# A decoder layer on one core: the gated half's normaliser moved behind its product, and two turned tiles read from PSUM

## The chip, the core and the metric

The kernel runs on one core of a Trainium2 chip. The core has a matrix engine (PE, TensorE), three engines for element-wise work (DVE or VectorE, ACT or ScalarE, POOL or GpSimd), a queue for transfers (SP) and 16 DMA engines. PE writes into PSUM, which has eight banks; the other data lies in SBUF. The engines run side by side, each takes its own list of instructions in order, and they wait for one another by semaphores.

The metric is device time in microseconds (us), as the median of several runs. All comparisons are on the same core.

## The reference, cut to what matters

Sequence 512, width 1024, one batch, one layer, float32 throughout. The mixing width is halved: 8 heads of block-sparse attention (512 columns) and a chunked gated unit (gMLP, 512 columns).

```
h = x @ w_in ; q, k, v, u, z = split(h)                 # u, z: 512 columns each
attn = moba_attention(rope(q), rope(k), v)
u, z = gelu(u), gelu(z)
sg = u * (tril(w_s) @ layer_norm(z) + b_s)              # spatial gating, chunks of 128
merged = concat(rms_norm(attn, attn_g), rms_norm(sg, gmlp_g))
x1 = layer_norm(ALPHA * x + merged @ w_out, ln1)        # ALPHA = 2 ** 0.25
ffn = (silu(x1 @ w_gate) * (x1 @ w_up)) @ w_down        # hidden 2816
out = layer_norm(ALPHA * x1 + ffn, ln2)
rms_norm(a, g) = a * rsqrt(mean(a ** 2) + 1e-6) * g     # over the 512 columns, per token
```

The normaliser of a token is one number. It can be multiplied into the token's row of `sg` before the product with `w_out`, or into the row of the product behind it; the gain `g` belongs to a column of `sg` and has to be in before.

## The kernel before

**Products.** Every float32 operand X is split into two parts of a faster matmul type: hi = X rounded (on ACT, L241) and lo = X - hi (on DVE or POOL, L242). A product is three matmuls, hi by hi, lo by hi and hi by lo (`mm3`, L252). Weights arrive by DMA as a tile `wr` of 128x1024 and are split into `wh` and `wl` by class `W` (L260). The table `WHI` names the weights whose hi part is made on DVE instead (L239), the table `WPOOL` those whose lo part is made on POOL. Names in these tables: `o0` to `o7` are the eight weight tiles of `w_out`, `q0` to `q3` those of the four pairs of heads, `z` those of the z projection.

**Order.** No instruction's place is written by hand. Functions only describe operations with their engine, a cost and the tiles they read and write; `Order.plan` (L110) then lists them. It walks a planned time forward, and whenever an engine comes free it takes, among the operations that are ready, the one with the smallest rank (`RANK`, with the place in the program as tie-break). Its costs, the handover between engines (`CROSS`), the ranks and the order of the parts (`SEQ`) are numbers at the top of the file. What comes out is one fixed list for each engine.

**Parts.** v first, then, by `SEQ`: `q0` to `q3` project and rotate (`qk_proj`, rope on DVE, SP and POOL), `a0` to `a3` are attention for two heads each, `z` and `u` project and apply GELU, `s` is the spatial unit. Projections fill PE while attention goes through DVE and ACT.

**The spatial unit (L554).** For each of four pairs of groups PE computes six small products into a bank `pj`, and DVE adds the bias and multiplies by u in place (L569, twice a pair, tile `ug`, tokens on partitions).

**The normaliser (`gmlp_norm`, L580).** For each of the four token tiles t: ACT squares the row and sums it (L587), DVE adds eps (L283), POOL takes the power -1/2 (L284), DVE scales the row by it and by the gain (L589), PE turns the 128x512 tile (four transposes, L594), and the turned tile is split into `znh` on ACT and `znl` on DVE (L241, L242). Only then can the product with the lower half of `w_out` begin for that t (`out_half(4, ...)`, L657). Its result is added to ALPHA times the residual `xk` (L651).

**Output product, attention's half (L784)** and the first LayerNorm: `pa_done` (L755) scales the product and adds it (L759), takes statistics (L696), POOL takes the power (L284), ACT normalises (L709), DVE multiplies the gain (L711), and the bias is added on POOL or DVE (L720) by the letter of `LN1` for the tile: "P" is POOL, "A" is DVE. Each half is turned by PE into a bank `tp` or `pv` (L769), copied by ACT into SBUF (`XR`, L773), and for some split from the bank.

**The feed-forward part** is a Strassen-like scheme: tiles 0 and 1 (`b11`, `b21`) are used alone in the first products of a pair (`p1`, `p2`), combinations of all four tiles (`n1`, `n2`, `t3`, `t4`, made in `combine`, L737) in the later ones. `p1` fills a bank and ACT copies it (L875) before `p2` adds to the same bank. Early weights get their lo part by a POOL-issued accumulating DMA (L250).

## Time and profile before

| | us |
|---|---|
| median of 3 runs (lowest to highest) | 559.56 (559.43 to 560.99) |
| the profiled execution | 557.63 |
| its span in the trace | 555.9 |
| PE busy in the span | 542.1 |
| DVE, ACT, POOL busy | 411.2, 285.8, 155.8 |

The span is the time from the first to the last instruction of the trace; the profiled execution's own time is 1.7 us longer. PE is the engine to look at: whatever its list waits for is time, and whatever the other engines do while it does not wait is not. PE works in a pipeline, so its rows overlap: the distance between two starts is what a matmul costs when nothing is waited for. The same holds, by less, for DVE and ACT.

### The profile page before, as it was taken

What the parts mean: (1) busy time and instruction counts of PE and PEld (TensorE: products, weight loads), DVE (VectorE), ACT (ScalarE), POOL (GpSimd) and SP (SyncE); (2) the same over time, 40 slices, a digit from 0 to 9 for tenths busy, and PEclk for the clock granted to TensorE, in tenths of its full rate; (3) what the DMA queues carried; (4) which work ended last, traced back from release to release, by engine and by line L of the source; (5) the groups of instructions that cost most, each with busy time, mean ns of one, the idle gap of its engine ahead of it and who ended that gap; (6) DMA issues with size and microseconds to landing.
All of it is one profiled execution on the core that took longest, in us unless ns stands there. A gap on an engine that the chain in (4) does not pass through costs nothing.

```text
span 555.9 us, 8789 instructions
## 1 busy us (share of the span) xinstructions
PE 542.1 (98%) x3360; PEld 484.7 (87%) x3360; DVE 411.2 (74%) x703; ACT 285.8 (51%) x488; POOL 155.8 (28%) x120
## 2 busy tenths in 40 slices
PE   9999999999899999999999999999999999999994
PEld 5888888888588899999999999999999888888883
DVE  5557779879986899989988878878877532324475
ACT  6323796788874698544454544454455332232211
POOL 0016248804203541144443324224233100000010
PEclk9999999999999999999999999999999999999998
DMA  7744423145723996344433233233223423223222
GB/s 249 257 156 150 137 70 101 52 155 174 259 58 115 268 220 193 121 146 152 151 114 116 77 114 115 80 130 98 73 77 122 143 78 113 85 105 100 90 75 75
DMA packets 22953, 71.80 MB, mean 129 GB/s; under 512 B 3072, under 2 KB 3584, under 8 KB 22912
## 3 DMA queue, kind: packets, MB, share of 16 engines
q1 hardware_dynamic: 22048, 68.11, 37.4%
q0 software_dynamic: 864, 3.15, 3.1%
q8 instruction: 26, 0.43, 0.3%
q14 instruction: 15, 0.12, 0.1%
HBM read 64.95 MB, written 2.10 MB: 121 GB/s over the span
## 4 chain that ended last, share of the span: by engine, by line
PE 95%; ACT 2%; DVE 1%; DMA 1%; issue 0%; DVEq 0%; ACTq 0%
PE pj L853 22%; PE sc L853 16%; PE pj L254 12%; PE pj L256 12%; PE pj L255 12%; PE sc L255 3%; PE sc L256 3%; PE sc L254 3%; PE pv L491 2%; PE tp L474 2%; PE sc L436 1%; PE pv L256 1%; PE tp L255 1%; PE pv L255 1%; PE tp L256 1%; PE pv L254 1%
## 5 line engine op out<-in xcount | busy, mean ns | idle before, releaser
L242 DVE TENSOR_TENSOR wl<-wr,wh 128x1024 fp32r<-128x1024 f32 (+1 forms) x56 | 69.9, 1249 | 62.1 <-ACT wh L241 61.7
L241 ACT ACTIVATE wh<-wr 128x1024 fp32r<-128x1024 f32 (+1 forms) x58 | 57.8, 999 | 84.2 <-PE sc L256 54.0
L853 PE MATMUL pj<-qk,wh 128*128 128x256 f32 x352 | 64.3, 283 | 0.0
L853 PE MATMUL sc<-xh,wh 128*128 128x256 f32 x352 | 64.3, 283 | 0.0
L284 POOL TENSOR_TENSOR sm<-sm,only 128x1 f32<-128x1 f32 (+2 forms) x17 | 16.9, 993 | 141.9 <-DVE sm L283 139.2
L853 PEld LDWEIGHTS pj<-qk,wh 128*128 128x128 f32 x352 | 54.9, 192 | 0.0
L853 PEld LDWEIGHTS sc<-xh,wh 128*128 128x128 f32 x352 | 54.9, 192 | 0.0
L853 PE MATMUL pj<-V,wh 128*128 128x256 f32 x288 | 52.9, 284 | 0.7 <-ACT cs L875 0.7
L853 PE MATMUL pj<-qk,wl 128*128 128x256 f32 x176 | 49.8, 283 | 0.0
L853 PE MATMUL sc<-xh,wl 128*128 128x256 f32 x176 | 49.8, 283 | 0.0
L254 PE MATMUL pj<-wh,xh 128*128 128x512 f32 x114 | 46.7, 410 | 0.0
L853 PEld LDWEIGHTS pj<-V,wh 128*128 128x128 f32 x288 | 44.9, 192 | 0.9 <-ACT cs L875 0.9
L255 PE MATMUL pj<-wl,xh 128*128 128x512 f32 x114 | 44.6, 391 | 0.0
L853 PE MATMUL pj<-V,wl 128*128 128x256 f32 x144 | 40.8, 284 | 0.0
L256 PE MATMUL pj<-wh,xl 128*128 128x512 f32 x96 | 37.8, 394 | 0.0
L242 POOL TENSOR_TENSOR wl<-wr,wh 128x1024 fp32r<-128x1024 f32 x7 | 17.2, 2459 | 73.4 <-ACT wh L241 50.6
L241 ACT ACTIVATE wh<-tp 128x512 fp32r<-128x512 f32 x33 | 19.7, 596 | 29.9 <-PE sc L853 20.4
L853 PEld LDWEIGHTS pj<-qk,wl 128*128 128x128 f32 x176 | 33.8, 192 | 0.0
L853 PEld LDWEIGHTS sc<-xh,wl 128*128 128x128 f32 x176 | 33.8, 192 | 0.0
L853 PE MATMUL sc<-ug,wh 128*128 128x256 f32 x176 | 32.3, 283 | 1.0 <-ACT wh L241 1.0
L242 DVE TENSOR_TENSOR wl<-tp,wh 128x512 fp32r<-128x512 f32 x33 | 22.6, 684 | 8.3 <-ACT wh L241 8.0
L853 PEld LDWEIGHTS sc<-ug,wh 128*128 128x128 f32 x176 | 27.5, 192 | 1.3 <-ACT wh L241 1.2
(349 smaller groups left out, 1511.0 us busy)
## 6 DMA issues: line engine op xcount, KB each, us to landing
wr<-w_dn SPq DMA_DIRECT2D x22, 512.0 KB, 3.3
wr<-w_gu SPq DMA_DIRECT2D x20, 512.0 KB, 4.1
zg<-w_gu SPq DMA_DIRECT2D x18, 512.0 KB, 3.3
kl<-w_gu SPq DMA_DIRECT2D x14, 512.0 KB, 3.3
wr<-w_vqk SPq DMA_DIRECT2D x8, 512.0 KB, 3.3
wr<-w_zu SPq DMA_DIRECT2D x8, 512.0 KB, 3.2
wr<-w_out SPq DMA_DIRECT2D x8, 512.0 KB, 4.3
wr<-w_vqk SPq DMA_DIRECT2D x8, 256.0 KB, 4.4
```

The costliest lines, as they stand in the source:

```text
L241: act(n, lambda: A.activation(hi(), src(), AF.Copy), rs, ws_hi, **k)
L242: either("P" if far else "D", n, lambda E: E.tensor_tensor(out=lo(), in0=src(), in1=hi().bitcast(F32), op=ALU.subtract), [*rs, *ws_hi], ws_lo,
L254: PE.matmul(o(), lhsT=lh(), rhs=rh(), start=start, stop=False)
L255: PE.matmul(o(), lhsT=lh(), rhs=rl(), start=False, stop=False)
L256: PE.matmul(o(), lhsT=ll(), rhs=rh(), start=False, stop=stop)
L284: od.op("POOL", 0.3 + 0.165 * n, lambda: PL.tensor_tensor(out=o.t, in0=v.t, in1=mhalf.t[:, :n], op=ALU.pow), [v, mhalf], [o], lock=True)
L436: PE.matmul(sc.t[:, :n], lhsT=qs.t[:, e, ts], rhs=ks.t[:, 2 * e + 1, :n], start=False, stop=True)
L474: PE.transpose(tp.t[:, j * P:j * P + P], p.t[:, j * P:j * P + P], ident.t)
L491: PE.matmul(pv.t[:, j * P:], lhsT=vs.t[:, j, h, :], rhs=pt.t[:, j * S:j * S + w], start=j == 0 and i == 0, stop=j == NT - 1 and i == 1)
L853: PE.matmul(o, lhsT=lh(w), rhs=buf.t[:, s + rh, x], start=first and side == k == i == 0, stop=k == 3 and i == 2, skip_group_check=True)
```

## The change

1. **Normaliser.** `gmlp_norm` goes. Right after each spatial pair j, `gmlp_turn(j)` turns the pair's 128 columns for all four token tiles (PE, L588), and splits them with the gain as a column scale: hi on ACT (L591), lo on DVE (L592). `gmlp_rms(t)` computes the sum of squares (ACT, L598) and the factor `rg` = 1 / (ALPHA rms) (DVE L601, POOL L603) beside that. The factor is applied behind the product: `xk` becomes product times `rg` plus the residual without ALPHA (L653). To fit, attention's factor `ra` also carries 1/ALPHA and the first LayerNorm's eps is divided by ALPHA squared. The gain moves from a row (`rowp`, 768 to 512 KB) to four columns (`colp`).
2. **PSUM.** For token tiles 2 and 3 `XR` is the bank itself: four copies (L773) go, and `combine` reads the banks `tp` and `pv`. It uses two SBUF tiles for n1 and n2 and computes t3 and t4 in place; the number of DVE operations in it stays.
3. **Tables.** `CROSS`, `SEQ`, `RANK`, `LNT`; `LN1` from "PAPA" to "PPPP" (bias of tiles 1 and 3 on POOL); `WHI` without `o1`, `o2` (hi part on ACT); `WPOOL` with `o5` and `q2` (lo part on POOL).

```diff
-SAME, CROSS, DMA_LAT, MM, MMD, MM256 = 0.15, 0.19, 1.9, 0.643, 0.681, 0.36
+SAME, CROSS, DMA_LAT, MM, MMD, MM256 = 0.15, 0.15, 1.9, 0.643, 0.681, 0.36
-SEQ = ('q1', 'a1', 'q0', 'z', 'q2', 'a0', 'u', 'q3', 's', 'a2', 'a3')
+SEQ = ('q1', 'q0', 'a1', 'z', 'q2', 'a0', 'u', 'a2', 'q3', 's', 'a3')
-LN1, LN2, LNT = "PAPA", "ADAD", 0.05
-WHI = ('o0', 'o1', 'o2', 'o3', 'q1')
-WPOOL = ('o1', 'o2', 'o4', 'z')
+LN1, LN2, LNT = "PPPP", "ADAD", 0.3
+WHI = ('o0', 'o3', 'q1')
+WPOOL = ('o1', 'o2', 'o4', 'o5', 'q2', 'z')
...
         for g2 in range(G // 2):
             pair(g2)
-    def gmlp_norm():
...
-            act(512, lambda: A.activation(sq.t, z(), AF.Square, accum_out=ss.t), [ug], [sq, ss], acc=True)
-            rsqrt_col(rs, lambda: ss.t, [ss], 1, 1.0 / 512, RMS_EPS)
-            dve(512, lambda: V.scalar_tensor_tensor(out=z(), in0=z(), scalar=rs.t, in1=rowp.t[:, 2, :], op0=ALU.mult,
-                                                    op1=ALU.mult), [rs, rowp, ug], [(ug, ("t", t))], lock=True)
...
+            gmlp_turn(g2)
+    sgh, sgl = [work([P, NT, S], tag, 1, F32R) for tag in ("znh", "znl")]
+    rg = small(NT)
+    def gmlp_turn(j):
+        tp, keys, g = pj(), [(ug, ("g", 2 * j)), (ug, ("g", 2 * j + 1))], lambda: colp.t[:, 12 + j:13 + j]
+        def turn():
+            for t in range(NT):
+                PE.transpose(tp.t[:, t * P:t * P + P], ug.t[:, t, j * P:j * P + P], ident.t)
+        pe(0.45, turn, [*keys, ident], [tp])
+        act(512, lambda: A.activation(sgh.t[:, j, :], tp.t, AF.Copy, scale=g()), [tp, colp], [(sgh, j)], aps=1)
+        dve(560, lambda: V.scalar_tensor_tensor(out=sgl.t[:, j, :], in0=tp.t, scalar=g(), in1=sgh.t[:, j, :].bitcast(F32),
+                                                op0=ALU.mult, op1=ALU.subtract), [tp, colp, (sgh, j)], [(sgl, j)])
+    def gmlp_rms(t):
+        sq, ss = tmp(), small(1)
+        act(512, lambda: A.activation(sq.t, ug.t[:, t, :], AF.Square, accum_out=ss.t), [ug], [sq, ss], acc=True,
+            base=RANK["sq2"])
...
-                dve(560, lambda: V.scalar_tensor_tensor(out=xk.t[:, t, hs], in0=xk.t[:, t, hs], scalar=ALPHA,
-                                                        in1=b[hf].t, op0=ALU.mult, op1=ALU.add),
+                dve(560, lambda: V.scalar_tensor_tensor(out=xk.t[:, t, hs], in0=b[hf].t, scalar=rg.t[:, t:t + 1],
+                                                        in1=xk.t[:, t, hs], op0=ALU.mult, op1=ALU.add),
...
-            xr = XR[i, t] = prob() if t < 2 else tmp()
-            act(512, lambda: A.activation(xr.t, tp.t, AF.Copy), [tp], [xr])
+            xr = XR[i, t] = prob() if t < 2 else tp
+            if t < 2:
+                act(512, lambda: A.activation(xr.t, tp.t, AF.Copy), [tp], [xr])
```

The lists of the engines move with it. PE's list holds the same 3358 matmuls before and after. It differs only in the stretch that ran from 49 to 245 us; before and behind that it is the same work in the same order (but for a few neighbours near the end).

PE, where the last of the spatial work meets the output product. Before: `tp_1533` is attention's turn, `pj_1541` and `pj_1585` are the turned tiles of t = 0 and 1, `pj_1566` is the output product of t = 0.

```order
L474 MATMUL tp_1533<-only_1_206,pr_1424 128x128 x3
L594 MATMUL pj_1541<-only_1_206,ug_1205 128x128 x4
L254 MATMUL pj_1566<-wh_1330,znh_1551 128x512
L255 MATMUL pj_1566<-wl_1358,znh_1551 128x512
L256 MATMUL pj_1566<-wh_1330,znl_1556 128x512
L254 MATMUL pj_1566<-wh_1408,znh_1551 128x512
L255 MATMUL pj_1566<-wl_1451,znh_1551 128x512
L256 MATMUL pj_1566<-wh_1408,znl_1556 128x512
L474 MATMUL tp_1582<-only_1_206,pr_1445 128x128
L594 MATMUL pj_1585<-only_1_206,ug_1205 128x128 x4
```

The same place now: `pj_1547` is the last spatial pair (its first three matmuls are its first group, the next three its second), `pj_1568` its turned columns, `pj_1581` the output product of t = 0.

```order
L474 MATMUL tp_1531<-only_1_208,pr_1391 128x128 x3
L254 MATMUL pj_1547<-znh_1000,wh_1271 128x256
L255 MATMUL pj_1547<-znl_1021,wh_1271 128x256
L256 MATMUL pj_1547<-znh_1000,wl_1376 128x256
L588 MATMUL pj_1568<-only_1_208,ug_1200 128x128 x4
L474 MATMUL tp_1576<-only_1_208,pr_1425 128x128
L254 MATMUL pj_1581<-wh_1389,znh_1561 128x512
L255 MATMUL pj_1581<-wl_1410,znh_1561 128x512
L256 MATMUL pj_1581<-wh_1389,znl_1574 128x512
```

The last spatial pair now stands directly ahead of the turn that needs it, and the turn directly ahead of the output product.

DVE at the same place. Before, from the first L589 on (`kl`, `rt`, `xh`, `atr`, `pr` belong to attention, `zg_1598` and `wl_1593` to the weights of `w_out`):

```order
L369 TENSOR_TENSOR rt_1512<-pj_1412,cs_199 128x512
L589 SCALAR_TENSOR_TENSOR ug_1205<-ug_1205,sm_1508,only_6_221 128x512
L462 RECIPROCAL sm_1528<-sm_1503 128x1
L370 TENSOR_TENSOR rt_1539<-pj_1412,cs_191 128x512
L668 SCALAR_TENSOR_TENSOR xh_1526<-atr_827,only_5_218,xh_1526 128x512 x2
L242 TENSOR_TENSOR znl_1556<-pj_1541,znh_1551 128x4x128
L283 TENSOR_SCALAR sm_1562<-sm_1547 128x1
L497 TENSOR_TENSOR atr_827<-atr_827,pv_1516 64x512
L242 TENSOR_TENSOR ptl_1573<-tp_1533,pth_1559 128x3x128
L589 SCALAR_TENSOR_TENSOR ug_1205<-ug_1205,sm_1570,only_6_221 128x512
L242 TENSOR_TENSOR wl_1593<-wr_1410,wh_1578 128x1024
```

Now (the L670 is the former L668):

```order
L450 ISA pr_1510,sm_1511<-sc_1440,only_2_213 128x256
L462 RECIPROCAL sm_1525<-sm_1507 128x1
L670 SCALAR_TENSOR_TENSOR xh_1495<-atr_726,only_5_220,xh_1495 128x512 x2
L370 TENSOR_TENSOR rt_1538<-pj_1327,cs_193 128x512
L462 RECIPROCAL sm_1544<-sm_1535 128x1
L409 TENSOR_TENSOR kl_1478<-rt_1364,kl_1478 64x512
L569 SCALAR_TENSOR_TENSOR ug_1200<-pj_1547,only_5_220,ug_1200 128x4x64
L497 TENSOR_TENSOR atr_726<-atr_726,pv_1515 64x512
L569 SCALAR_TENSOR_TENSOR ug_1200<-pj_1547,only_5_220,ug_1200 128x4x64
L242 TENSOR_TENSOR ptl_1566<-tp_1531,pth_1542 128x3x128
L592 SCALAR_TENSOR_TENSOR znl_1574<-pj_1429,only_5_220,znh_1561 128x512
L592 SCALAR_TENSOR_TENSOR znl_1574<-pj_1451,only_5_220,znh_1561 128x512
```

L589 and the wide `wl` are out of the way (that `wl` is on POOL now), and the last pair's two L569 stand behind attention's rows.

PE at the start of the feed-forward part, where `p2` of pair 2 (bank `pj_2347` before) begins. Before, `p2` of pair 1 (`pj_2257`) stood ahead of it:

```order
L853 MATMUL pj_2257<-V_2153,ptl_2026 128x256 x2
L853 MATMUL pj_2257<-V_2153,znl_2012 128x256
L853 MATMUL pj_2347<-V_2153,wh_2211 128x256 x2
L853 MATMUL pj_2347<-V_2153,wl_2224 128x256
```

Now the last rows of `p1` of that pair (`pj_2348`, weights `wh_2152`) stand three matmuls of pair 3 (`pj_2439`) ahead of its `p2` (weights `wh_2227`):

```order
L859 MATMUL pj_2348<-V_2141,wh_2152 128x256 x2
L859 MATMUL pj_2348<-V_2141,wl_2169 128x256
L859 MATMUL pj_2439<-V_2141,wh_2266 128x256 x2
L859 MATMUL pj_2439<-V_2141,wl_2276 128x256
L859 MATMUL pj_2348<-V_2141,wh_2227 128x256 x2
L859 MATMUL pj_2348<-V_2141,wl_2242 128x256
```

Between the end of `p1` and the start of `p2` on one bank there were 16 rows of another pair before, and there are two now.

POOL at the same time. Before:

```order
L284 TENSOR_TENSOR sm_2112<-sm_2109,only_7_73 128x1
L720 TENSOR_TENSOR xl_1510<-xl_1510,kl_1822 128x512 x2
L250 DMA wl_2173<-w_gu 128x1024
L284 TENSOR_TENSOR sm_2233<-sm_2229,only_7_73 128x1
L250 DMA wl_2224<-w_gu 128x1024
L284 TENSOR_TENSOR sm_2273<-sm_2267,only_7_73 128x1
L720 TENSOR_TENSOR xl_1510<-xl_1510,kl_1822 128x512 x2
L250 DMA wl_2284<-w_gu 128x1024
```

Now:

```order
L284 TENSOR_TENSOR sm_2105<-sm_2102,only_7_73 128x1
L722 TENSOR_TENSOR xl_1497<-xl_1497,kl_1828 128x512 x4
L250 DMA wl_2169<-w_gu 128x1024
L284 TENSOR_TENSOR sm_2200<-sm_2187,only_7_73 128x1
L722 TENSOR_TENSOR xl_1497<-xl_1497,kl_1828 128x512 x2
L250 DMA wl_2242<-w_gu 128x1024
L284 TENSOR_TENSOR sm_2295<-sm_2286,only_7_73 128x1
L250 DMA wl_2276<-w_gu 128x1024
L722 TENSOR_TENSOR xl_1497<-xl_1497,kl_1828 128x512 x2
```

The bias of all four tiles is on POOL, and that of the last tile stands behind a DMA issue.

## Rows read from the trace of the kernel before

**Rows 1.** Busy time by stretch: width, then busy us and (instructions) of each engine.

```profile
core 0: us, PE busy (x) PEld busy (x) DVE busy (x) ACT busy (x) POOL busy (x), PEclk, DMA share, GB/s
40.00:130.00 90.00, 90.00 (x457) 76.07 (x456) 71.39 (x175) 64.19 (x123) 48.32 (x32) 1.00 0.36 110
...
140.00:150.00 10.00, 7.26 (x34) 5.06 (x34) 9.53 (x17) 9.84 (x20) 2.40 (x3) 1.00 0.82 268
...
220.00:230.00 10.00, 9.31 (x76) 9.03 (x76) 9.94 (x17) 5.33 (x10) 2.40 (x1) 1.00 0.20 57
...
250.00:540.00 290.00, 290.00 (x1979) 270.64 (x1978) 200.77 (x256) 120.56 (x186) 67.75 (x51) 1.00 0.32 105
```

**Rows 2.** Waits of PE: total us, times, longest.

```profile
PE pj L255 <- DVE sm L283: 1.3, 1, 1.3
...
PE sc L853 <- ACT wh L241: 1.0, 1, 1.0
PE pj L254 <- ACT znh L241: 1.0, 1, 1.0
PE pj L853 <- ACT cs L875: 0.7, 1, 0.7
PE pj L594 <- DVE ug L589: 0.3, 1, 0.3
```

**Rows 3.** Timeline, 141 to 146 us: start, duration, engine, line, tile.

```profile
141.91 0.50 PE L256 MATMUL pj<-wh,znl 128*128 128x512 f32 x1
...
144.11 1.81 DVE L242 TENSOR_TENSOR wl<-wr,wh 128x1024 fp32r<-128x1024 f32 x1 [0.47 <-ACT wh L241]
...
145.97 0.50 PE L255 MATMUL pj<-wl,znh 128*128 128x512 f32 x1 [1.34 <-DVE sm L283]
```

**Rows 4.** Timeline of DVE, 130 to 143 us.

```profile
130.53 0.48 DVE L569 SCALAR_TENSOR_TENSOR ug<-pj,only,ug 128x256 f32<-128x256 f32 x1
130.93 0.55 DVE L242 TENSOR_TENSOR ptl<-tp,pth 128x384 fp32r<-128x384 f32 x1
...
139.85 1.40 DVE L668 SCALAR_TENSOR_TENSOR xh<-atr,only,xh 128x512 fp32r<-128x512 f32 x2
141.18 0.68 DVE L242 TENSOR_TENSOR znl<-pj,znh 128x512 fp32r<-128x512 f32 x1
```

**Rows 5.** Timeline of PE, 129 to 132 us.

```profile
129.64 0.28 PE L254 MATMUL pj<-znh,wh 128*128 128x256 f32 x1
...
130.00 0.28 PE L254 MATMUL pj<-znh,wh 128*128 128x256 f32 x1
```

**Rows 6.** Timeline of PE around 224 and 240 us.

```profile
223.78 0.28 PE L853 MATMUL pj<-V,wl 128*128 128x256 f32 x1
224.75 0.50 PE L853 MATMUL pj<-V,wh 128*128 128x256 f32 x2 [0.69 <-ACT cs L875]
...
239.27 0.28 PE L853 MATMUL sc<-xh,wl 128*128 128x256 f32 x1
240.56 0.48 PE L853 MATMUL sc<-ug,wh 128*128 128x256 f32 x2 [1.01 <-ACT wh L241]
```

**Rows 7.** Timeline of POOL, 205 to 210 us.

```profile
206.80 2.70 POOL L720 TENSOR_TENSOR xl<-xl,kl 128x512 f32<-128x512 f32 x2
209.45 0.87 POOL L250 DMA_DIRECT2D wl<-w_gu  x1
```

**Rows 8.** Timeline of DVE and POOL where they meet, 50 to 54 and 204 to 208 us.

```profile
50.31 2.39 POOL L242 TENSOR_TENSOR wl<-wr,wh 128x1024 fp32r<-128x1024 f32 x1 [0.93 <-ACT wh L241]
...
50.78 2.46 DVE L403 TENSOR_TENSOR qk<-rt,qk 64x512 fp32r<-64x512 f32 x1 [0.60 <-ACT qk L402]
...
53.34 0.69 DVE L403 TENSOR_TENSOR qk<-rt,qk 64x512 fp32r<-64x512 f32 x1
...
204.44 0.15 DVE L700 SCALAR_TENSOR_TENSOR sm<-sm,sm 128x1 f32<-128x1 f32 x1
...
207.02 1.26 DVE L700 SCALAR_TENSOR_TENSOR sm<-sm,sm 128x1 f32<-128x1 f32 x1
```

More of the change, by code (lines that the diff above doesn't have):

```diff
@@ L576, in spatial @@
             pair(g2)
-    SG = {}
-    def gmlp_norm():
-        sgh, sgl = work([P, NT, S], "znh", 1, F32R), work([P, NT, S], "znl", 1, F32R)
-        def one(t):
-            ts = slice(t * P, t * P + P)
-            z = lambda: ug.t[:, t, :]
-            sq, ss, rs, tp = tmp(), small(1), small(1), pj()
-            act(512, lambda: A.activation(sq.t, z(), AF.Square, accum_out=ss.t), [ug], [sq, ss], acc=True)
-            rsqrt_col(rs, lambda: ss.t, [ss], 1, 1.0 / 512, RMS_EPS)
-            dve(512, lambda: V.scalar_tensor_tensor(out=z(), in0=z(), scalar=rs.t, in1=rowp.t[:, 2, :], op0=ALU.mult,
-                                                    op1=ALU.mult), [rs, rowp, ug], [(ug, ("t", t))], lock=True)
-            def turn():
-                for j in range(4):
-                    PE.transpose(tp.t[:, j * P:j * P + P], ug.t[:, t, j * P:j * P + P], ident.t)
-            pe(0.45, turn, [(ug, ("t", t)), ident], [tp])
-            split(512, lambda: tp.t.rearrange("p (j c) -> p j c", c=P), lambda: sgh.t[:, :, ts],
-                  lambda: sgl.t[:, :, ts], [tp], [(sgh, t)], [(sgl, t)], lock=False)
-        for t in range(NT):
-            one(t)
-        SG[0] = (sgh, sgl)
+            gmlp_turn(g2)
@@ new lines, in gmlp_rms @@
+    def gmlp_rms(t):
+        sq, ss = tmp(), small(1)
+        act(512, lambda: A.activation(sq.t, ug.t[:, t, :], AF.Square, accum_out=ss.t), [ug], [sq, ss], acc=True,
+            base=RANK["sq2"])
+        v = small(1)
+        dve(1, lambda: V.tensor_scalar(v.t, ss.t, ALPHA ** 2 / 512, ALPHA ** 2 * RMS_EPS, op0=ALU.mult, op1=ALU.add),
+            [ss], [v], base=RANK["sq2"])
+        od.op("POOL", 0.465, lambda: PL.tensor_tensor(out=rg.t[:, t:t + 1], in0=v.t, in1=mhalf.t[:, :1], op=ALU.pow),
+              [v, mhalf], [(rg, t)], lock=True, base=RANK["sq2"])
@@ L612, in s_part @@
         spatial()
-        gmlp_norm()
+        for t in range(NT):
+            gmlp_rms(t)
     parts = {"z": z_part, "u": lambda: gelu(ug, tok_proj(4)), "s": s_part}
@@ L686, in build, with layer_norm @@
     HV = [slice(0, 512), slice(512, 1024)]
-    def layer_norm(t, add, done, how):
+    def layer_norm(t, add, done, how, eps=LN_EPS):
         keys = [(xk, (t, 0)), (xk, (t, 1))]
@@ L780, in pa_done @@
         od.base = RANK["ln"] + LNT * t
-        layer_norm(t, add, done, LN1[t])
+        layer_norm(t, add, done, LN1[t], LN_EPS / ALPHA ** 2)
         od.base = RANK["fill"]
```

48 lines of the change are left out of this document (25 added, 23 removed).

## The prediction, made before the changed kernel was run

> **What bounds the kernel now.** I read the busy time by stretch first, to see where PE does not work. It is busy for 90.00 of 90 us from 40 to 130 us and for 290.00 of 290 from 250 to 540 [rows 1]. The change moves nothing behind 245 us, so nothing can be won or lost there but by carrying a delay along. In the stretch that the change touches, PE is short only from 140 to 150 us, 7.26 of 10, and by a little from 220 on, as 9.31 of 10 [rows 1]. Second come the waits of PE [rows 2]: 1.3, 1.0 and 0.3 us belong to the 140s, 0.7 and 1.0 to the start of the feed-forward part. Idle time alone is too small a count, since PE's rows also stretch: at 141.91 a matmul stands 0.5 us behind the one before it, because its `znl` was just being made. By start distances beyond the usual 0.227 us per matmul, my working from the whole stretch gives 4.2 us lost from 140 to 150, against the 2.74 that are idle [rows 1]. From 220 to 245 it gives 2.3: 0.85 between 223.78 and 224.75 (0.97 less the usual 0.12), 1.17 between 239.27 and 240.56, and 0.3 in small pieces [rows 6].
>
> So at most 4.2 + 2.3 = 6.5 us can come back, out of 557.63. The profile says in the same row what else holds the 140s: DVE is busy for 9.53 and ACT for 9.84 of 10 us there [rows 1]. That the normaliser's chain stands in PE's way is true, but the engines behind it are full.
>
> **The normaliser.** Off the path go four L589 and the three operations ahead of each. PE still needs the turned tile and its split. What takes the chain's place is the last spatial pair: bias and gate on DVE (L569), turn, hi on ACT, lo on DVE, then the product. I walked DVE's new list from the first L569 to the eighth, on which the last turn waits. It holds eight L569 at 0.40 (start to start, [rows 4]), two L670 at 0.665 (the pair of 1.33, 139.85 to 141.18, [rows 4]), two L409, L369, L370, L497 and one whole-width `ptl` at about 0.6 like the other whole-width rows, and some fifteen shorter rows of attention that come to 2.8 in all: 3.2 + 1.3 + 3.7 + 2.8 = 11.0 us. PE has between the end of the first group of products and that turn: seven groups at 0.36 [rows 5] or 2.5, three projection products at 0.68 or 2.0, 1.3 for three turns of `ug`, 1.1 for attention's turns, 0.7 for scores and 1.2 for a `mix`: 8.8 us. DVE is late by 11.0 - 8.8 = 2.2, with handovers 2.35. Before it, PE waits some 0.8 for attention's own `pth` and `tp`, behind it some 0.4, among that 0.15 for the `wl` of `o5`, which POOL now makes in 2.39 [rows 8] and DVE made in 1.81 [rows 3]. Sum 3.6 against 4.2: **-0.6 us**. The wait is turned over from ACT, POOL and DVE in a row to DVE alone. Bounds: DVE's rows of attention could slip behind the last L569 no further, since the list is fixed, but the walk's sum is off by a tenth either way, and ACT's four L591 in a row could come 1 us late. I take -2.5 to +1.0.
>
> The rest of the normaliser is hidden. L598, L601 and L603 come behind, POOL's power of one column takes about what it did, and `rg` is needed only when the first product of t = 0 is done, eight products later. L653 has as many operands as L651. The smaller DMA for `rowp` lands long before z is normalised. If that cover were gone, the price were one chain, ACT to POOL, once.
>
> **PSUM.** Four ACT copies of some 0.5 go. ACT at 204 to 214 is full, so they are worth having there, but PE did not wait for `n1` and the others: combine ran some 2.4 us ahead of its products. The banks `tp` and `pv` are kept longer, until `n1` and `n2` are made; the turns of tile 3 stand further back now and that covers it. I take 0, between -0.5 and +0.5. A whole-width DVE row that reads a bank takes 0.68 [rows 4] and one that reads SBUF alone 0.69 [rows 8], so the source adds nothing that I can see.
>
> **The start of the feed-forward part.** Two things get worse. The bias of tiles 1 and 3 moves from DVE, where it took some 0.65 each, to POOL at 2.70 for two [rows 7], and for tile 3 behind a DMA issue of 0.87 [rows 7]: I count 0.4 us for a turn that waits. And `p2` of pair 2 comes three matmuls behind its `p1` instead of sixteen rows. The place at 224 us shows what a `p2` directly behind its `p1` costs, 0.85 [rows 6]. Of that the three matmuls cover 0.36, which leaves 0.5 if ACT is free. The other two waits stay: pair 3 has the same 0.85, and the one at 240.56 comes to about 1.05 against 1.17. Sum: 0.4 + 0.5 - 0.1 = **+0.8 us**, between -0.5 (the turns aren't late, and ACT's copy is out in time) and +2.0 (both and ACT behind by another copy).
>
> **Order of attention.** From 49 to 130 us PE waits for nothing today [rows 1]. In the new list the scores of the first attention come some 4.7 us earlier against their chain of POOL's add, ACT and DVE's split and a transfer. I get 2 us of slack there and 0.8 at one weight later. I take 0, between -0 and +1.5, as there is nothing to win.
>
> **Sum.** 557.63 - 0.6 + 0 + 0.8 + 0 = 557.8. The profiled execution lies 1.93 under the median of 559.56, so the forecast is 559.8.
>
> **Rivals.** First, the chain really was the wait and DVE's queue is not one: the eighth L569 is out in time, PE loses some 1 us where it lost 4.2, and the start of the feed-forward part comes to nothing: 559.56 - 3.2 = 556.4. If the later waits go too, 554.5. For it: the whole ACT, DVE, POOL, DVE, PE, ACT loop is gone, DVE has 9.7 us less to do in all, and the turns for the first three pairs are done while attention still runs. Against it: DVE's share of 9.53 [rows 1], and that the new list puts L670, L370 and L409 ahead of the last pair.
>
> Second, slower: POOL's added work holds DVE. At 50.78 a DVE row of two SBUF tiles took 2.46 us beside POOL's L242, and 0.69 for the next one without it; at 207.02 a row of one column took 1.26 beside POOL's L720, and 0.15 without [rows 7, 8]. The change gives POOL three more L242 and four more bias additions in the first LayerNorm. Each can hold such a DVE row, by 1.77 and by 1.11. It decides where PE waits for DVE, which is at the last spatial pair (one low half) and in the LayerNorm (two more pairs of additions): 1.77 + 2 x 1.11 = 4.0, of which I take three quarters as uncovered, 3.0, as 559.8 + 3.0 = 562.8. Against it: L569 and L592 read a bank and only one SBUF tile, so that only L670, L409 and the like are hit.
>
> [...]
>
> Third, the same side with another mechanism: the scores of the first attention come before their transfer, 1 to 1.5 us at most, 561. It lies within the range.
>
> **How the numbers follow.** A run of this kernel can be told from no change by about 0.3%, or 1.7 us. My forecast (wait turned over, +-1.7 around 559.8, cut at the same bound) gets 0.43. The first rival gets 0.35, since the walk's term of 2.35 is a difference of two sums of 11 and 9. The second gets 0.17 and the third 0.05 beyond the bound. So faster 0.35, within 0.3% 0.43, slower 0.22. The range runs from 555.3, with the better part of the first rival in it, to 562.4, which leaves out some 0.1 on each side.
>
> **What will show it.** PE's busy share in the stretch of the last L588: 7 of 10 if I am right, over 9 if the first rival is. The wait of PE L588 on DVE L569 should be near 2 us, with L670, L370 and L409 in DVE's timeline directly ahead of it without a gap. At the start of the feed-forward part the wait for the copy `cs` (now L881) should stand twice, 0.5 and 0.7. If DVE rows of 1.2 to 2.5 us stand beside POOL's L242 or L722 ahead of a wait of PE, it is the second rival. The forecast is wrong if L588 does not wait, or if waits arise from 49 to 130 us.

## The result, and the profile after

The changed kernel takes 563.69 us (median of four runs, 563.28 to 565.04). The kernel before, run beside it, takes 559.98 (559.43 to 560.99). The ratio is 1.0071, with an interval of 1.0053 to 1.0088: 3.7 us slower, where no change was forecast. The range ended at 562.4, so the time lies outside it, and the side it came out on had been given a chance of 0.22. The versions further down were each run beside the kernel before, at other times than the changed kernel, so that their ratios to it compare better than their times. One run in all, of the version with two mends, took 672.07 at a mean clock of 0.75, a slow state, and is left out of its median.

The profiled execution of after took 563.28, its span is 561.6, against 557.63 and 555.9 before: the two traces differ by 5.7 us, the medians by 3.7. The trace of before is of an execution 2.3 us under its median, that of after of one 0.4 under. So the traces are good for finding places and sizes, and 2 us of their difference is not the change's.

The page's list of busy times, engine by engine:

```profile
PE 545.4 (97%) x3360; PEld 486.5 (87%) x3360; DVE 404.4 (72%) x690; ACT 285.8 (51%) x486; POOL 169.0 (30%) x127
```

DVE has 6.8 us less to do than before (411.2), ACT the same, POOL 13.2 more (155.8). PE is busy for 3.3 us longer with the same products. That is the first sign: an engine whose work is the same is busier only if single rows take longer or overlap less, as behind the wait at 144.00, where an L254 takes 0.38 that takes 0.28 elsewhere [rows 5].

The waits of PE in after, as total us, times, longest (before: [rows 2]):

```profile
PE pj L859 <- ACT cs L881: 2.0, 3, 0.9
PE pj L588 <- DVE ug L569: 1.6, 1, 1.6
...
PE pj L254 <- DVE rt L370: 0.7, 1, 0.7
PE tp L474 <- DVE ptl L242: 0.7, 2, 0.5
PE pv L491 <- ACT pth L241: 0.5, 1, 0.5
```

Counted as the prediction counts (start distances beyond the usual ones, my working over the whole trace), PE loses 18.3 us in after and 12.6 in before. The difference of 5.7 is the whole difference of the spans, and it lies in these places (where a stretch is cut moves up to 0.3 between neighbours):

| stretch | before | after | difference | forecast |
|---|---|---|---|---|
| first 10 us | 1.2 | 1.6 | +0.4 | 0 |
| 80 to 100 us, attention | 0.5 | 1.1 | +0.6 | 0 (0 to +1.5) |
| 130 to 160 us, spatial unit and output product | 5.5 | 7.65 | +2.15 | -0.6 (-2.5 to +1.0) |
| 200 to 250 us, start of the feed-forward part | 2.75 | 5.4 | +2.65 | +0.8 (-0.5 to +2.0) |
| all the rest | 2.65 | 2.55 | -0.1 | 0 |

Behind 250 us nothing is lost, as before: PE is busy for 280.00 of 280 us from 260 to 540.

**The spatial unit.** The timeline of PE, 144 to 151 us (start, duration, engine, line, tile, and in brackets the idle time ahead and what ended it):

```profile
144.00 0.38 PE L254 MATMUL pj<-znh,wh 128*128 128x256 f32 x1 [0.74 <-DVE rt L370]
...
146.53 0.66 PE L588 MATMUL pj<-only,ug 128*128 128x128 f32 x4 [1.56 <-DVE ug L569]
...
147.65 0.79 PE L254 MATMUL pj<-wh,znh 128*128 128x512 f32 x1 [0.16 <-DVE znl L592]
148.24 0.63 PE L255 MATMUL pj<-wl,znh 128*128 128x512 f32 x1
148.67 0.63 PE L256 MATMUL pj<-wh,znl 128*128 128x512 f32 x1
...
150.69 0.39 PE L255 MATMUL pj<-wl,znh 128*128 128x512 f32 x1
150.92 0.40 PE L256 MATMUL pj<-wh,znl 128*128 128x512 f32 x1
```

And that of DVE behind which PE waits:

```profile
137.50 0.88 DVE L569 SCALAR_TENSOR_TENSOR ug<-pj,only,ug 128x256 f32<-128x256 f32 x2 [0.88 <-PE pj L256]
...
141.95 1.40 DVE L670 SCALAR_TENSOR_TENSOR xh<-atr,only,xh 128x512 fp32r<-128x512 f32 x2
143.26 0.68 DVE L370 TENSOR_TENSOR rt<-pj,cs 128x512 f32<-128x512 f32 x1
...
144.04 0.69 DVE L409 TENSOR_TENSOR kl<-rt,kl 64x512 fp32r<-64x512 f32 x1
145.00 0.48 DVE L569 SCALAR_TENSOR_TENSOR ug<-pj,only,ug 128x256 f32<-128x256 f32 x1 [0.28 <-PE pj L256]
...
146.00 0.47 DVE L569 SCALAR_TENSOR_TENSOR ug<-pj,only,ug 128x256 f32<-128x256 f32 x1
...
146.86 2.71 DVE L592 SCALAR_TENSOR_TENSOR znl<-pj,only,znh 128x512 fp32r<-128x512 f32 x4
```

L670, L370 and L409 stand in a row from 141.95 to 144.73 ahead of the last pair's L569, as the walk had it. But they do not hold that L569. Behind them DVE stands idle for 0.28 and waits for PE's last product of the pair. What they hold is PE, which does not start the pair until 144.00, when L370 has ended. By that it needed the bank that L370 was still reading: each turned tile keeps a `pj` bank until its L592, and the four L592 come only behind the last L569. So 0.91 is lost ahead of the pair, to DVE's queue. The 1.72 ahead of the turn are mostly the pair's own road: PE's list puts the turn behind the pair with nothing between, and both L569 (0.41 and 0.47) have to come first. Of DVE's queue only L497 stands between them, with 0.59.

Then the windows. They give width, then busy us and (instructions) of PE, PEld, DVE, ACT and POOL, then the granted clock, the DMA share and GB/s:

```profile
140.00:144.00 4.00, 2.49 (x14) 1.73 (x14) 3.99 (x12) 3.77 (x9) 0.00 (x0) 1.00 0.60 180
144.00:147.00 3.00, 1.44 (x10) 1.18 (x10) 2.69 (x7) 2.98 (x6) 0.90 (x1) 1.00 0.81 243
147.00:148.00 1.00, 0.84 (x4) 0.49 (x3) 1.00 (x2) 1.00 (x3) 1.00 (x1) 0.56 0.93 340
148.00:150.00 2.00, 2.00 (x6) 1.52 (x6) 2.00 (x6) 2.00 (x6) 1.82 (x3) 0.50 0.92 311
150.00:151.00 1.00, 1.00 (x5) 0.82 (x4) 1.00 (x2) 0.97 (x3) 0.47 (x1) 0.73 0.67 229
140.00:150.00 10.00, 6.77 (x30) 4.92 (x31) 9.69 (x24) 9.74 (x21) 3.71 (x3) 0.86 0.76 241
```

From about 147.1 to 150.5 the granted clock is 0.50. In PE's rows it is the distance of 0.43 between products that otherwise stand 0.23 apart (148.24 to 148.67, against 150.69 to 150.92). The six distances from 147.65 to 150.37 take 2.72 us where six of 0.227 take 1.36: about 1.4 us. (Some expectations below still count eight products and 1.6.) In the trace of before the same ten microseconds have a clock of 1.00 [rows 1]. Of the +2.15 in this stretch, then, about 1.4 are the clock and 0.8 are waits.

**The start of the feed-forward part.** PE's three waits for the copy between two products on one bank:

```profile
218.97 0.50 PE L859 MATMUL pj<-V,ptl 128*128 128x256 f32 x2 [0.61 <-ACT cs L881]
...
224.50 0.51 PE L859 MATMUL pj<-V,wh 128*128 128x256 f32 x2 [0.47 <-ACT cs L881]
...
231.03 0.50 PE L859 MATMUL pj<-V,wh 128*128 128x256 f32 x2 [0.87 <-ACT cs L881]
```

By starts they cost 0.77, 0.63 and 1.03. Before there was one such wait, 0.85 [rows 6]. The first is new altogether. ACT, ahead of it:

```profile
214.19 1.51 ACT L711 ACTIVATE xl<-xl,sm,sm 128x512 f32<-128x512 f32 x2
215.71 1.28 ACT L886 ACT_TABLE_LOAD   x1
217.00 0.38 ACT L886 ACTIVATE sqa<-pj 128x256 f32<-128x256 f32 x1
217.28 0.62 ACT L241 ACTIVATE xh<-pr 128x512 fp32r<-128x512 f32 x1
217.81 0.62 ACT L241 ACTIVATE ug<-pr 128x512 fp32r<-128x512 f32 x1
218.33 0.59 ACT L881 ACTIVATE cs<-pj 128x512 f32<-128x512 f32 x1
```

The last product of that `p1` ended at 216.20. Its copy starts 2.1 us later. Behind the normalising of two half tiles (L711, done at 215.70) ACT loads a table, applies SiLU to a half tile (both L886) and makes two splits, in a row without a gap. The twelve rows of PE between `p1` and `p2`, 18 matmuls in 2.2 us, did not cover that.

### The profile page after: what moved, and what is told of

Read it like the earlier page. It is cut to its first block, busy times and chain, and to the rows that moved or that the text cites. A ratio compares the mean times of both kernels' runs of the same rounds, so it can differ in the third digit from the quotient of the medians.

```text
span 561.6 us, 8778 instructions
## 1 busy us (share of the span) xinstructions
PE 545.4 (97%) x3360; PEld 486.5 (87%) x3360; DVE 404.4 (72%) x690; ACT 285.8 (51%) x486; POOL 169.0 (30%) x127
## 4 chain that ended last, share of the span: by engine, by line
PE 89%; DVE 5%; ACT 2%; DMA 2%; issue 1%; POOL 1%; DVEq 0%; ACTq 0%
PE pj L859 20%; PE sc L859 17%; PE pj L254 11%; PE pj L256 11%; PE pj L255 11%; PE sc L255 2%; PE sc L256 2%; PE sc L254 2%; DMA wr<-w_gu 2%; PE tp L474 1%; PE pv L491 1%; PE sc L435 1%; PE sc L436 1%; PE pv L256 1%; PE tp L255 1%; PE pv L255 1%
## 5 line engine op out<-in xcount | busy, mean ns | idle before, releaser
L242 DVE TENSOR_TENSOR wl<-wr,wh 128x1024 fp32r<-128x1024 f32 (+1 forms) x53 | 65.4, 1234 | 19.4 <-ACT wh L241 19.0
L241 ACT ACTIVATE wh<-wr 128x1024 fp32r<-128x1024 f32 (+1 forms) x60 | 59.8, 997 | 38.1 <-PE sc L255 7.2
L284 POOL TENSOR_TENSOR sm<-sm,only 128x1 f32<-128x1 f32 (+2 forms) x13 | 14.9, 1148 | 127.2 <-DVE sm L283 127.1
L254 PE MATMUL pj<-wh,xh 128*128 128x512 f32 x114 | 47.1, 413 | 0.0
L242 POOL TENSOR_TENSOR wl<-wr,wh 128x1024 fp32r<-128x1024 f32 x10 | 23.9, 2398 | 45.9 <-ACT wh L241 30.1
L241 ACT ACTIVATE wh<-tp 128x512 fp32r<-128x512 f32 x33 | 19.7, 596 | 30.3 <-PE sc L859 20.4
L242 DVE TENSOR_TENSOR wl<-tp,wh 128x512 fp32r<-128x512 f32 x33 | 22.6, 684 | 8.3 <-ACT wh L241 7.8
```

The lines of the kernel that those rows point to most:

```text
L241: act(n, lambda: A.activation(hi(), src(), AF.Copy), rs, ws_hi, **k)
L242: either("P" if far else "D", n, lambda E: E.tensor_tensor(out=lo(), in0=src(), in1=hi().bitcast(F32), op=ALU.subtract), [*rs, *ws_hi], ws_lo,
L254: PE.matmul(o(), lhsT=lh(), rhs=rh(), start=start, stop=False)
L284: od.op("POOL", 0.3 + 0.165 * n, lambda: PL.tensor_tensor(out=o.t, in0=v.t, in1=mhalf.t[:, :n], op=ALU.pow), [v, mhalf], [o], lock=True)
```

## The experiments

The theory after the two traces was: (a) the idle time at 140 to 146.5 us is DVE's queue, as the walk had it, and the lower clock behind it adds to the cost; (b) the start of the feed-forward part pays for copies that ACT makes late. The rivals: the tables alone are bad; the PSUM part is the cost; POOL's added work holds DVE; and whatever wait is removed, the next queue takes it over.

### New code with the old tables

The code of after, with `CROSS`, `SEQ`, `RANK` (and 10.0 for the new entry `sq2`), `LNT`, `LN1`, `WHI`, `WPOOL` of before.

> The changed code (normaliser behind the product, tiles 2 and 3 read from PSUM) under the tables of before (CROSS, SEQ, RANK, LN1, LNT, WHI, WPOOL; the new rank sq2 set to 10.0). Theory A, the loss sits in where the tables put things: this is level with or faster than before, 556 to 560 us, the waits at 219, 231 and 246 us of the changed kernel shrink to about 2 us in all, and PE's granted clock does not fall. Theory B, the loss sits in the code (the last spatial pair waits for DVE's queue whatever the tables): 562 to 564 us, a wait of PE on L569 of 1.5 us or more, and a clock below 1.00 behind it.

570.56 us, ratio 1.0186 (1.0166 to 1.0207). The clock stays at 1.00 from 130 to 160 us, though the turn waits just as long (1.6); PE is busier around it, 8.09 us from 140 to 150 against 6.77 in after. The loss lies elsewhere, at the first LayerNorm. Waits of PE:

```profile
PE tp L774 <- ACT xl L711: 4.1, 1, 4.1
...
PE tp L774 <- POOL xl L722: 1.5, 1, 1.5
```

Neither theory had these two waits of L774. Behind the longer one the clock falls here too: its mean from 207 to 214 us is 0.51. What follows is that the new code does not come out faster with the old numbers either, and that one wait's length does not settle whether the clock falls.

### Old code with the new tables

> The code of before under the new tables. Theory A (tables): 562 to 565 us, with the waits for the copy cs at the start of the feed-forward part as in the changed kernel, 2 us. Theory B (code): 559 to 561 us. If both halves lose, it is worse than before by about half of 3.7 us, near 562.

575.76 us, ratio 1.028 (1.025 to 1.0309). Waits of PE:

```profile
PE tp L474 <- DVE ptl L242: 7.4, 5, 2.7
```

The window of 140 to 160 us:

```profile
140.00:160.00 20.00, 12.99 (x48) 10.34 (x48) 16.43 (x33) 14.78 (x32) 4.59 (x6) 0.66 0.66 221
```

Attention's turns wait five times, and the clock is 0.66 on average. It falls twice more, to means of 0.57 from 214 to 222 us and 0.51 from 259 to 266. The tables cost 15.8 us on the old code, the code 10.6 on the old tables, both together 3.7. They belong to each other, and neither half alone tells what the other is worth.

### The PSUM part alone

The kernel before, with the two turned tiles read from their banks and the new `combine`.

> Before with tiles 2 and 3 read from PSUM and nothing else changed. My forecast put this at 0 with bounds of -0.5 and +0.5 us: 559.5 to 560.5 us. A rival says that banks tp and pv held longer make the turns of tile 3 wait: +0.5 to +1.5 us, with a wait of PE on DVE at about 212 us.

561.29 us, ratio 1.0018 (1.0005 to 1.0031): about 1.0 us slower, where 0 was forecast. `p2` now waits twice for its copy, and a turn waits 0.84 at 202.51 for a split on DVE. That turn is of the second tile. The banks that are held longer come in only with the four turns from 211.31 to 216.55, and none of these waits. Ahead of the split ACT had stood idle before a weight's hi part (timeline of ACT):

```profile
199.70 1.06 ACT L248 ACTIVATE wh<-wr 128x1024 fp32r<-128x1024 f32 x1 [1.11 <-PE pj L255]
```

Waits of PE:

```profile
PE pj L857 <- ACT cs L879: 1.4, 2, 0.7
...
PE pv L772 <- DVE V L242: 0.8, 1, 0.8
```

The lists of the 140s read as those of before, and yet the clock fell there in this execution, as the window shows:

```profile
140.00:150.00 10.00, 7.45 (x26) 5.23 (x27) 9.45 (x17) 9.68 (x20) 2.55 (x3) 0.83 0.81 266
```

So a part of the 1.0 us may be the clock, and not the banks.

### All but the PSUM part

Its complement: the changed kernel with the four copies and the `combine` of before.

> The changed kernel without its PSUM part: tiles 2 and 3 copied to SBUF by ACT (L773 of before) and combine as before; new normaliser and new tables. By e4, where the PSUM part alone cost 1.0 us (interval 0.3 to 1.7), it should win about 1 us: 562.7. If the tables only fit the lists with the PSUM part, it loses: 564 to 567.

563.16 us, ratio 1.0058 (1.0036 to 1.008), 0.5 under after. `L588` waits 1.6 here too, `cs` twice, 0.9 in all. The interval overlaps that of after, so 0.5 cannot be told from nothing. By the medians of these two versions the PSUM part carries 0.5 to 1.0 of the 3.7 (0 to 1.7 with the intervals), and the normaliser with its tables the rest.

### Filling the idle time, in the turn's own bank

Six more matmuls, whose result nobody reads, ahead of the last turn.

```diff
         def turn():
+            if j == 3:
+                for _ in range(6):
+                    PE.matmul(tp.t, lhsT=vs.t[:, 0, 0, :], rhs=vs.t[:, 0, 0:4, :], start=True, stop=True)
             for t in range(NT):
```

> The changed kernel with six more matmuls of 512 columns (1.4 us at full clock) into the bank of the last turn of ug, ahead of that turn, in the time in which PE waits for L569; the turn overwrites them, and every other instruction stands as it did. Theory: the granted clock of 0.50 from 147.3 to 150.4 us follows from that idle time, so with PE busy the clock stays at 1.00 and the eight matmuls that were 0.2 us late each are on time: 1.6 us less, about 562.0 us. Rival: the clock falls anyway, or the added matmuls delay the turn by as much: 563.5 us or more.

566.75 us, ratio 1.0117 (1.0098 to 1.0136). A miss, and an instructive one: the bank is freed only with L569, so that the fill waited where the turn had waited, and then ran itself at the lower clock (timeline of PE).

```profile
145.78 2.93 PE L589 MATMUL pj<-V 128*128 128x512 f32 x6 [1.56 <-DVE ug L569]
```

Five distances in 2.93 less the last row's 0.63 are 0.46 each, nearly the distance of the slow products above. The clock had begun to fall during the wait itself: 0.80 is the mean from 145 to 146 us, and 0.50 from 146 to 149. From 149 on it is 1.00 again, but the six had been added to the path. Later a score product (L435) waits 2.3 us for a transfer, which no wait in after corresponds to.

### Filling it in a free bank

The same six matmuls in a bank that is free, behind the last spatial pair.

```diff
+            if more:
+                spare = bank("sc", 2)
+                def fill():
+                    for _ in range(6):
+                        PE.matmul(spare.t, lhsT=vs.t[:, 0, 0, :], rhs=vs.t[:, 0, 0:4, :], start=True, stop=True)
+                pe(0.01, fill, [m, vs], [spare], base=-30)
```

> The changed kernel with six more matmuls of 512 columns into a bank sc that is free, behind the last spatial pair and ahead of the turn L588, with no wait of their own; every other instruction stands as it did. In e6 the added matmuls waited with the turn for L569, as their bank was the one that L569 reads, so they filled nothing. Theory: the granted clock of 0.50 behind L588 follows from PE's idle time ahead of it. With the 1.7 us of waiting filled, the clock stays at 1.00 and 1.6 us come back: 562.1 us against 563.7. Rival: the clock falls for what PE did over a longer stretch (the waits at 140, 141 and 144 us count too), and the fill changes nothing: 563.7, or 565 if the fill itself runs at half clock.

The windows:

```profile
144.00:147.00 3.00, 2.83 (x17) 2.12 (x17) 2.71 (x6) 2.98 (x7) 0.99 (x1) 1.00 0.81 251
147.00:148.00 1.00, 0.74 (x4) 0.50 (x4) 1.00 (x2) 1.00 (x3) 1.00 (x1) 1.00 1.06 410
148.00:150.00 2.00, 2.00 (x11) 1.58 (x10) 2.00 (x6) 2.00 (x6) 1.83 (x3) 1.00 0.85 262
```

With the idle time filled the clock stays at 1.00 there, and 11 rows stand from 148 to 150 where there were 6. The time is nevertheless 564.74 (562.86 to 567.42), ratio 1.0081 (1.0054 to 1.0107), no better than after. In the profiled execution, the slowest of the six, what the clock gave back went to other waits of PE:

```profile
PE sc L435 <- DMA qk<-qk: 2.4, 2, 2.1
```

The longer is a score product at 158.64. In after PE starts it at 157.78 without a wait. So 1.2 of the 2.1 us are PE coming sooner, and 0.9 the transfer landing later than that. And behind this wait the clock falls after all:

```profile
156.00:159.00 3.00, 0.89 (x5) 0.49 (x4) 0.26 (x1) 0.00 (x0) 0.00 (x0) 1.00 0.84 193
...
160.00:163.00 3.00, 3.00 (x11) 2.71 (x10) 1.48 (x6) 1.45 (x6) 0.00 (x0) 0.52 0.02 7
```

In this execution the idle time and the fall behind it had moved, not gone. Why the transfer lands later, and whether the five quicker executions show the same, is open.

### DVE's rows out of the way

Attention's second scaling (L670) is made to depend on the last L569, so that the planner puts it behind.

```diff
-        ak = [(atr, (f, 0)), (atr, (f, 1)), colp]
+        ak = [(atr, (f, 0)), (atr, (f, 1)), colp, (ug, ("g", 7))]
```

> The changed kernel with one more dependency: the split of attention's first outputs (L666 on ACT, L670 on DVE) comes only behind the last L569. It moves 1.33 us of DVE and 1.2 of ACT from ahead of L370 and the last two L569 to behind them. Theory (DVE's queue is what the last turn waits for): the waits at 144.0 for L370 and at 146.5 for L569 shrink by 1.3 us together, and with them the drop of the clock may go, 1.6 us more: 561 to 562.4 us. Rival (another engine is next, as ACT at 9.74 of 10): no change, 563.7.

561.97 us, ratio 1.0038 (1.0022 to 1.0054): 1.7 under after. The waits for L370 and L569 are gone. What stands in their place, by the waits of PE:

```profile
PE pj L254 <- DVE znl L592: 1.5, 1, 1.5
```

The window of the 140s:

```profile
140.00:150.00 10.00, 7.24 (x38) 5.38 (x38) 9.67 (x21) 9.29 (x18) 3.67 (x2) 1.00 0.75 247
```

DVE is as full as before (9.67 of 10) and PE as idle as in before (7.24 against 7.26 [rows 1]). The wait went from one operation of DVE's queue to the next. Most of what is gained in this stretch is the clock, 1.00 here: the slow products had cost about 1.4. The mean granted clock of its ten runs is 0.995 to 0.998, that of after's four 0.993 to 0.996. The two traces differ by 0.7 only, and the two intervals touch, so the size is an agreement, not a measurement of the clock.

### The copy `cs` first

```diff
-            act(512, lambda: A.activation(self.a.t, self.X.t, AF.Copy), [self.X], [self.a], base=EVAC)
+            act(512, lambda: A.activation(self.a.t, self.X.t, AF.Copy), [self.X], [self.a], base=-30)
```

> The changed kernel with the copy of p1's bank (L881 on ACT) ranked ahead of all else on its engine; it changes eight places of ACT's list at the start of the feed-forward part, and the order of six matmuls there on PE. Theory: the waits of PE for cs at 219.0 and 224.5 us (0.77 and 0.63) go, 1.4 us: 562.3 us. Rival: the copy is late because p1 ends late and the split that it overtakes is then waited for: 563.7.

564.79 us, ratio 1.0089 (1.007 to 1.0109); not better. The waits for it are 2.3 us in three (2.0 in after). The copy passes two splits, but the two L711, the table load and SiLU still stand ahead of it: it starts directly behind the SiLU, at 218.42. The planner, thinking the copy done earlier, moved `p2` forward as well. A higher rank did not make room here; it moved the consumer too.

### Both: DVE's rows behind, and the copy's true latency

The edit on L670, and the planner told that the copy takes 0.8 longer before its consumer may go (`base=EVAC, lat=0.8`).

> f6 (attention's first outputs split behind the last L569) and, besides, the planner is told that the copy of p1's bank takes 0.8 us longer to reach PE, so that it puts more rows of other pairs between p1 and p2: eight for pair 1's first half more, six matmuls instead of three ahead of pair 2's p2. Theory: the waits for cs of 0.77 and 0.63 us go, 1.2 us under f6: 560.8 us. Rival: the wait turns into one for the turns of tiles 2 and 3, which move with it: 562.

560.76 us, ratio 1.0013 (1.0003 to 1.0024). This is the best of the changed versions: 2.9 of the 3.7 us are regained, by the ratios 0.58 of the 0.71%. Waits of PE:

```profile
PE pj L254 <- DVE znl L592: 1.5, 1, 1.5
PE pv L774 <- DVE sm L699: 1.4, 1, 1.4
```

Of the three waits for a copy one is left, 1.0. The turn at 203.01 waits 1.38 on a chain that begins on ACT, which stands in its list before a weight that has not arrived (timeline of ACT):

```profile
200.11 1.06 ACT L248 ACTIVATE wh<-wr 128x1024 fp32r<-128x1024 f32 x1 [1.12 <-DMA wr<-w_gu]
```

In before the same L248 runs at 197.21 without a wait.

### The third copy, by PE's order

The last version, with a later product of another pair put between `p1` and `p2` of pair 3 (`lat=2.5` for that pair alone).

> f9 with one more move, on PE alone: the first product of pair 0's second kind (p5) now stands between p1 and p2 of pair 3, where p2 stood directly behind. No other engine's list changes. Theory (a p2 directly behind its p1 costs the copy's whole latency): the wait of 1.2 us at 228.9 goes, 559.9 us, level with before. Rival (p5's operands n1 are late, or the weight's split): the wait only changes its name, 561.

561.24 us, ratio 1.0026 (1.0012 to 1.0041), the same as the one above. The wait for `cs` is gone, and PE waits for the weights of the product that was put there, 0.6 for `wh` and 0.4 for `wl`.

### The turned tile's split ahead of the weight

If ACT's wait for the weight is what delays the turn at 203 us, the split of the turned tile (L241) ought to go first. The hi part of that weight is made to depend on it, once on the last version and once on after.

```diff
-  lambda: b.hi(c), lambda: b.lo(c), [raw.key], [b.hk], [b.lk], base=PREP)
+  lambda: b.hi(c), lambda: b.lo(c), [raw.key, *([(tv, (2, 0)), (tv, (3, 0))] if early == 4 else [])], [b.hk], [b.lk], base=PREP)
```

> f12 with the hi part of an early weight (L248 of pair 2) placed on ACT behind the split of tile 0's second half, where it stood ahead of it. Theory: in f9 ACT stood 1.1 us at 200 us waiting for the transfer of that weight, with the split behind it that frees bank pv, and PE's turn into pv waited 1.5 us at 203; with the split ahead that wait goes: 558.5 us, below before. Rival: the turn is late for POOL's bias (2.93 us for two) all the same, or the weight is then late for its product: 560 to 561.

567.01 us, ratio 1.012 (1.0102 to 1.0138). The turn no longer waits. The weight's hi part does (timeline of ACT):

```profile
204.08 1.06 ACT L248 ACTIVATE wh<-wr 128x1024 fp32r<-128x1024 f32 x1 [3.99 <-DMA wr<-w_gu]
```

And PE waits for what stands behind it, 3.3 for a split on ACT and 2.2 for a token tile whose bias comes late from POOL.

> The changed kernel with that one placing on ACT alone (L248 of pair 2 behind the split of tile 0's second half); the planner moves what hangs on it. Theory: the wait at 204.3 us, 0.53, goes and, with p5 now between p1 and p2 of pair 3, that of 1.03 at 231: 562.2 us. Rival: PE is held by p2 behind p1 of the other pairs, 563.7.

570.68 us, ratio 1.018 (1.016 to 1.02), with 2.7 us for `cs` in two waits and 2.1 for a split. These two are 5.8 and 7.0 us slower than the versions they were made from. Behind their long waits the clock falls too, in both twice beyond 200 us (means of 0.57 from 208 to 212 and 0.66 from 221 to 226 in the first), and that is part of the price. ACT's list still holds a row that waits for a weight, and with that row put later the products that need the weight come later as well.

### Two tiles' bias back on DVE

`LN1` "PAPA" instead of "PPPP", on after.

> The changed kernel with the bias of tiles 1 and 3 back on DVE (LN1 PAPA), all else as changed. Theory (the bias on POOL delays the turns): the waits at 204.3 and 210.0 us, 0.53 and 0.28, go and nothing else moves: 562.9 us. Rival (what counts is where p2 stands behind p1, which this reshuffles): anything from 562 to 565.

565.89 us, ratio 1.0096 (1.0081 to 1.0112): slower than after by 2.2. The waits are others (`sc` on a weight 2.3, `pv` on a split 1.1). So putting the bias back does not win the time; since the lists move with it, what the bias on POOL costs by itself is not shown.

### The kernel before, a second profile

> The kernel before, once more, for a second trace. The first trace is of an execution of 557.63 us, 2.3 under the median of its runs, and shows a granted clock of 1.00 from 140 to 150 us. Theory: the stall there lies at the edge at which the clock falls, so that another execution of the same lists shows a clock below 1.00 behind 146 us and is 1.5 us longer, 559 to 561 us. Rival: the clock stays at 1.00 and the spread comes from elsewhere, as from the first 10 us.

557.90 us, span 556.2. The theory had been that the trace of before, 2 us under the median, was an execution in which the clock happened not to fall, and that another would show the fall. It did not, by the window of the 140s:

```profile
140.00:150.00 10.00, 7.30 (x34) 4.90 (x33) 9.52 (x18) 9.84 (x20) 2.92 (x3) 1.00 0.80 278
```

But this execution, too, was one of the quicker ones, so that it does not speak of the others. Over the runs of before beside all these kernels, the 33 with a mean granted clock of 0.996 or more have a median of 559.7, the 27 with 0.994 or 0.995 one of 560.4, and the 7 below that 560.4 too. That hints at a share of the clock in before's own spread, and is no more than a hint.

## Why the prediction was wrong

Three steps of the sum failed. The start of the feed-forward part was put at +0.8 and measures +2.65; the largest single piece is a `p2` behind a late copy, which was not in the sum. The waits at the normaliser were put at 3.6 and measure 4.96. And the lower clock behind them had no term and cost 1.4.

**What bounds the kernel: right.** The waits are where it looked, the engines behind the normaliser's chain were full, and nothing is won or lost behind 250 us.

**The normaliser: mechanism right in part, size off, and a second cost missed.** PE's busy share from 140 to 150 us is 6.77 of 10, where 7 was named for the forecast and over 9 for the first rival. The wait was handed from ACT, POOL and DVE in a row to DVE, and the rows that were named stand where they were named. The walk gave 2.35 for it; it is 0.91 + 1.72 = 2.63, the first part in the form of a bank that DVE had not freed. That the two totals agree is partly luck. The walk took DVE's list for one that never waits, and PE's for one that only waits at its end. From the first L569 (133.27) to the end of the eighth (146.47) DVE took 13.2 us, not 11.0, and waited for PE's own products in it, 0.88 ahead of 137.50 and 0.28 ahead of 145.00. So the gap that was forecast not to be there is there, and most of the wait at the turn is the last pair's passage through L569. Attention's own waits ahead of it were put at 0.8 and are 0.31 + 0.69 + 0.64 + 0.23 = 1.87 (at 134.21, 140.30, 141.18 and directly behind). Behind the turn 0.46 were lost to `znl`, against 0.4. The step that failed is the sum of 3.6: these add to 1.87 + 2.63 + 0.46 = 4.96. That is 0.8 more than the 4.2 of before, and not 0.6 less.

The second cost, 1.4 us of lower clock, was in no bound. The prediction read the granted clock of 1.00 in before's 140s [rows 1] and took it for granted that a wait of about the same total would leave it there. With the idle time filled the clock stayed up there, and fell at 159.5 behind the next wait; with the fill stuck behind the same wait it fell, and before the fill began. Of all the profiles, the six that have the waits of after from 140 to 147 us show the fall (means from 140 to 150 us: 0.86 in after, 0.88 without the PSUM part, 0.83 with the fill in the turn's bank, 0.88 with the copy first, 0.92 with two tiles' bias on DVE, 0.89 with the split first). The four with L670 moved show none there. These runs bear the theory out that the idle time brings the fall. But in the new code with the old tables it did not fall behind the same 1.6 us wait, with PE busier around it, and in the PSUM part alone it fell with the lists of before, to a mean of 0.83 where both traces of before show 1.00. From which idle time on it falls cannot be said from these runs, and two of after's four runs have a mean clock (0.995, 0.996) at which it may not have fallen.

**PSUM: perhaps too low.** Forecast 0, between -0.5 and +0.5; alone it costs 1.0 (0.3 to 1.7), and within the change 0.5, which cannot be told from nothing. Even the 1.0 is not all its own, as the clock fell in that profile. The cover that was named for the longer-held banks held: the turns of tiles 2 and 3 waited for nothing there. The turn that waited 0.84 came ahead of them.

**The start of the feed-forward part: the term that was mis-sized most.** Of its three parts, the turns were put at 0.4 and measure 0.53 (204.26, behind statistics on DVE) and 0.28 (209.98, behind the bias on POOL), 0.8 in all. `p2` of pair 2 was put at 0.5 and measures 0.63. The -0.1 for pair 3 and the later weight is +0.18 - 0.14, about nothing. What is missing from the sum is `p2` of pair 1, 0.77: twelve rows of PE stood between it and its `p1`, and I took that for cover without walking ACT's list, in which 2.1 us of other work stood ahead of the copy once `p1` had ended. With pieces of 0.1 behind each of these waits it makes +2.65 for +0.8. The bound of +2.0 named "both and ACT behind by another copy"; ACT was behind by a table load, a SiLU and two splits, with a LayerNorm ahead of them.

**Order of attention: about right.** One wait at 90.58 and its follow-ups, 0.6, within 0 to +1.5. It is a turn that waits for a split on DVE, and not the scores behind their transfer, which the third rival named.

**The sum.** Forecast +0.2; the places give 0.4 + 0.6 + 2.15 + 2.65 - 0.1 = 5.7 between the traces and 3.7 between the medians. The profiled execution of before was taken as lying 1.93 under its median with the same offset for after; after's lies 0.4 under. Where the 2 us of before's median over its trace come from stays open.

**The rivals.** The first fell with the busy share of 6.77: L588 does wait. The second had the right side and not the mechanism. DVE rows that take longer beside a row of POOL can be seen, as this pair from the timelines of POOL and DVE, 1.77 us where the same form takes 0.68 at 214.48:

```profile
217.06 3.35 POOL L722 TENSOR_TENSOR xl<-xl,kl 128x512 f32<-128x512 f32 x2 [3.50 <-DVE xl L713]
```

```profile
219.19 1.77 DVE L242 TENSOR_TENSOR ug<-pr,ug 128x512 fp32r<-128x512 f32 x1
```

But no wait of PE of any size stands behind them, and taking two bias additions from POOL made the kernel slower (565.89 against 563.69). In the 140s, POOL's L242 and L374 run from 146.10 to 149.72 beside the four L592, which take 2.71 together, 0.68 each: not held. They read a bank and one SBUF tile. So does L569, which in before took 0.48 at 127.20 and at 128.19 beside POOL's L242 (126.66 to 129.08), as it did at 130.53 without one [rows 4]; an L409, of two SBUF tiles, took 2.74 at 45.48 beside such an L242 (44.87 to 47.68), and 0.69 as the median of its eight. What came nearest in the feed-forward part is named only in a bound, as "ACT behind by another copy": ACT's list at the start of the feed-forward part.

**Whether the change could have paid.** With the two worst places mended it comes to 560.76, still 0.13% over before (0.03 to 0.24%). What remains is DVE's queue in the 140s (1.5 us for L592) and a turn behind ACT and a transfer at 200 us. Why ACT finds the weight late there was not separated: in this version the two early weights ahead of it are split 2.2 and 2.3 us later than before (185.23 and 191.15 against 183.06 and 188.83), PE's turns there come 1.2 later (196.60 against 195.44), and the DMA share from 190 to 200 us is about 1 in both kernels. No version beat the kernel before.
